# Strassen's products for the first six chunks of the down projections of a two-layer decoder trunk

## The chip, the cores and the metric

The kernel runs on one core of one Trainium2 chip. The metric is device microseconds (us) of one execution, as the median of several runs. The changed kernel is compared with the kernel before on the same chip. Engines are called PE (TensorE, matrix products), ACT (ScalarE), DVE (VectorE), POOL (GpSimd) and SP (SyncE, which issues the loads).

## The reference

Two layers (L = 2) act on x of 256 tokens by 1024 channels, in fp32. Each layer is an FFN, a token mixing and a second FFN, with a layer norm behind each. The change touches the FFNs alone, four in all:

```python
def swiglu(x, w_gate, w_up, w_down):
    return (jax.nn.silu(x @ w_gate) * (x @ w_up)) @ w_down
...
    for l in range(DEPTH):
        x = layer_norm(ALPHA * x + 0.5 * swiglu(x, ffn1_gate[l], ffn1_up[l], ffn1_down[l]),
                       ln1_g[l], ln1_b[l])
        ...
        x = layer_norm(ALPHA * x + 0.5 * swiglu(x, ffn2_gate[l], ffn2_up[l], ffn2_down[l]),
                       ln3_g[l], ln3_b[l])
```

The FFN's hidden width is 2816, so w_down is 2816 by 1024.

## The kernel before

**Precision.** Every fp32 operand a of a large product is split into a rounded part hi and a rest lo, both of type float32r. A product is then three matmuls (`mm3`, L185 to L187): hi with hi, hi with lo, lo with hi. ACT makes hi by a cast (L162 for weights, L200 for activations), DVE makes lo by a subtraction (L163, L200).

**Weights.** All weights come in one stream of tiles of 128 x 1024 in the order of a plan. `ensure` loads the next tile into one of five `raw` buffers (SP issues the load), splits it into one of twelve `hi` and one of twelve `lo` buffers, and runs seven tiles ahead of the tile that PE asks for.

**An FFN.** The hidden width is cut into a chunk 0 of 512 and chunks 1 to 9 of 256. For chunk 0, gate and up are computed with tokens on the partitions (`tok`: 128 x 512 matmuls for each half t of the tokens), then h = silu(gate) * up is transposed on PE (`trans`, tile `tr`). For chunks 1 to 9, `chan` computes gate (`pg`) and up (`pu`) with the channels on the partitions, 48 matmuls of 128 x 256 each; ACT makes `sg` = silu(pg) (L350), DVE makes h = pu * sg (L355), and h is split into `hTh` and `hTl`. `down` adds a chunk's share of h @ w_down to four PSUM tiles `y` (two halves of the tokens by two halves of the 1024 output columns): for each block of 128 hidden rows 2 x 2 products of 128 x 512, three matmuls each.

**Order.** A scheduler fixes each engine's order of instructions when the program is built. Within the step of chunk c, PE computes gate c, then a share of the down projection of earlier chunks, then up c. The down share of a step is 24 matmuls in most steps; chunks 6 to 9 are taken at the end of the FFN. In the trace each engine's instructions start in that order, so one that waits holds up those behind it.

**PSUM.** There are eight banks: two for `gu` (gate and up take turns), two for `tr`, four for `y`.

Of the kernel before, what the change touches and what calls it, by code (L numbers as in the profile page):

```python
# [7 lines left out]
F32 = mybir.dt.float32  # L8
F32R = mybir.dt.float32r
# [8 lines left out]
S = 256  # L18
# [5 lines left out]


CHUNKS = [(0, 512)] + [(512 + 256 * i, 256) for i in range(9)]


def _w_in_groups():
# [92 lines left out]
def _build(tc, A, out):  # L122
# [3 lines left out]
    with ExitStack() as es:  # L126
# [6 lines left out]
        sm = pool("sm", 3)  # L133
        lnp = pool("lnp", 1)
        ps = pool("ps", 2, space=PSUM)


        plan = _plan()
# [6 lines left out]
        loaded = []  # L145
        splits = []
        stream = []

        def ensure(i):
# [177 lines left out]
        def ffn(l, f, lni, last=False, mid=None):  # L327
            n = len(CHUNKS)
            y = {}
            started = set()  # L330
            products = []

            def tok(name, t, tag="gu", bufs=2, ahead=None):

                w = kslices((l, f, name, 0), 512, ahead)
                p = ps.tile([128, 512], F32, name="p" + name, tag=tag, bufs=bufs)
                products[:] = [mm3(p, xT(t, k), w[k], k == 0, k == KC - 1) for k in range(KC)]
                return p

            def chan(name, c):  # L340

                w = kslices((l, f, name, c), 256)
                p = ps.tile([128, 2, 256], F32, name="p" + name, tag="gu")
                proj_chan(p, w, 0)
                return p


            def gated(p):
                sg = wk.tile([128, 512], F32, name="sg", tag="w")
                ACT.activation(sg, p.rearrange("p a b -> p (a b)") if len(p.shape) == 3 else p, AF.Silu)  # L350
                return sg

            def product(p, sg):
                h = wk.tile([128, 512], F32, name="h", tag="w")
                DVE.tensor_tensor(h, p.rearrange("p a b -> p (a b)") if len(p.shape) == 3 else p, sg, ALU.mult)  # L355
                return h

            hT = {}

            def hpair():  # L360
                return (wk.tile([128, 512], F32R, name="hTh", tag="a"),
                        wk.tile([128, 512], F32R, name="hTl", tag="a"))

            def trans(h, t):
                tr = ps.tile([128, 512], F32, name="tr", tag="tr")
                for i in range(4):
                    c = slice(i * 128, i * 128 + 128)
                    PE.transpose(tr[:, c], h[:, c], ident)
                hT[0, t] = hpair()
                split_to(*hT[0, t], tr)  # L370

            def stationary(c, t, i):
                if c == 0:
                    s = slice(i * 128, i * 128 + 128)
                    a = hT[0, t]
                else:
                    s = slice(i * 256 + t * 128, i * 256 + t * 128 + 128)
                    a = hT[c]
                return a[0][:, s], a[1][:, s]

            def down(cs, t, end=False):

                todo = [(c, i, nn) for c in cs for i in range(CHUNKS[c][1] // 128) for nn in range(2)]
                if end:
                    todo.sort(key=lambda v: v[2])
                if t not in y:
                    y[t] = [ps.tile([128, 512], F32, name="y", tag="y", bufs=4) for _ in range(2)]
                done = []
                for j, (c, i, nn) in enumerate(todo):
                    hi, lo = blocks((l, f, "d", c))[i]  # L390
                    s = slice(nn * 512, nn * 512 + 512)
                    stop = end and (j == len(todo) - 1 or todo[j + 1][2] != nn)
                    done.append(mm3(y[t][nn], stationary(c, t, i), (hi[:, s], lo[:, s]), (t, nn) not in started, stop))
                    started.add((t, nn))
                return done

            h = {}
            if l == 0 and f == 1:
                sg = [gated(tok("g", 0, "y", 4, ahead=0))]
# [4 lines left out]
                sg.append(gated(tok("g", 1, "y", 4)))  # L404
                h = {t: product(tok("u", t), sg[t]) for t in range(2)}
                trans(h[0], 0)
            else:
                for t in range(2):
                    sg = gated(tok("g", t))
                    if t == 1:  # L410
                        trans(h[0], 0)
                    h[t] = product(tok("u", t), sg)


            late = 4
            for c in range(1, n):
                p = chan("g", c)
                sg = gated(p)
                if c == 1:
                    trans(h[1], 1)  # L420
                    down([0], 0)
                elif c == 2:
                    down([0], 1)
                    down([1], 0)
                else:
                    if c - 2 < n - late:
                        down([c - 2], 1)
                    if c - 1 < n - late:
                        down([c - 1], 0)
                hc = product(chan("u", c), sg)  # L430
                hT[c] = hpair()
                split_to(*hT[c], hc)
                if c == 2:
                    with tc.issue_after(stream[-1].ins):
                        gb = load_ln(l, lni)
                if c == 4 and mid:
                    with tc.issue_after(stream[-1].ins):
                        mid()
            down(range(n - late, n - 1), 0)
            down([n - 1], 0, end=True)  # L440
            done = down(range(n - late, n), 1, end=True)
            layer_norm(0, y[0], 2 * ALPHA, 4 * EPS, gb, last, [done[9], done[14]])
            layer_norm(1, y[1], 2 * ALPHA, 4 * EPS, gb, last)


        def mixing(l, sp):
            gbn = load_ln(l, 1)

            def token_proj(key, n, t):
                w = kslices((l, key), n)  # L450
                p = ps.tile([128, 512], F32, name="pt", tag="gu")
                for k in range(KC):
                    mm3(p[:, :n], xT(t, k), w[k], k == 0, k == KC - 1)
                return p

            def chan_proj(key, n, b0, ahead=None):

                w = kslices((l, key), n, ahead)
                p = ps.tile([128, 2, 256], F32, name="pc", tag="gu")
                proj_chan(p, w, b0)  # L460
                return p

# [101 lines left out]
            mixl = [lop.tile([128, 8, 128], F32R, name="mixl", tag="lo") for _ in range(2)]  # L564

            def spatial():
                p = ps.tile([128, 2, 2, 128], F32, name="psv", tag="gu")
# [38 lines left out]

            yo = {}

            def w_out(t, kbs, tag, bufs, by_half):
                w = blocks((l, "wo"))  # L610
                if t not in yo:
                    yo[t] = [ps.tile([128, 512], F32, name="yo", tag=tag, bufs=bufs) for _ in range(2)]
# [117 lines left out]
            with ExitStack() as order:  # L730
# [3 lines left out]
                for i, (t, slots) in enumerate(steps):  # L734
# [14 lines left out]
                w_out(0, range(4), "gu", 2, False)  # L749
                w_out(0, range(4, 8), "gu", 2, True)  # L750
                heads_out(1)
                layer_norm(0, yo[0], ALPHA, EPS, gbn)
                w_out(1, range(8), "y", 4, True)
                layer_norm(1, yo[1], ALPHA, EPS, gbn)

        for l in range(L):
# [41 lines left out]
```

## Time and profile before

| | |
|---|---|
| median of 3 runs | 994.37 us (994.21 to 994.58) |
| the profiled execution, its own time | 993.1 us |
| its span, first to last instruction | 991.4 us |
| PE busy | 978.0 us, 99% of the span |
| DVE busy | 603.2 us, 61% |
| ACT busy | 468.4 us, 47% |
| granted TensorE clock, mean | 0.997 of full speed |

The profiled execution is 1.27 us faster than the median of the runs, and its time is 1.7 us more than its span. A busy share is the time in which an engine has some instruction in work; matmuls overlap one another, so PE's speed is read from the spacing of matmuls, not from their durations.

### The profile page before, as it was taken

What the parts mean: (1) busy time and instruction counts of PE and PEld (TensorE: products, weight loads), DVE (VectorE), ACT (ScalarE), POOL (GpSimd) and SP (SyncE); (2) the same over time, 40 slices, a digit from 0 to 9 for tenths busy, and PEclk for the clock granted to TensorE, in tenths of its full rate; (3) what the DMA queues carried; (4) which work ended last, traced back from release to release, by engine and by line L of the source; (5) the groups of instructions that cost most, each with busy time, mean ns of one, the idle gap of its engine ahead of it and who ended that gap; (6) DMA issues with size and microseconds to landing.
All of it is one profiled execution on the core that took longest, in us unless ns stands there. A gap on an engine that the chain in (4) does not pass through costs nothing.

```text
span 991.4 us, 16634 instructions
## 1 busy us (share of the span) xinstructions
PE 978.0 (99%) x6824; PEld 887.4 (90%) x6828; DVE 603.2 (61%) x830; ACT 468.4 (47%) x658; POOL 19.7 (2%) x42
## 2 busy tenths in 40 slices
PE   7999999999999999999999999999999999999996
PEld 6999999899878899999889999998988789999995
DVE  6655455686769555455584545548678785545534
ACT  6644444256655444344354444434565663534420
POOL 1000000010000000000000000000000000000000
PEclk9999999999999999999999999999999999999998
DMA  8967565385226666556375766554642265755601
GB/s 284 331 241 237 171 198 187 105 309 160 87 86 194 231 213 194 189 189 205 94 231 195 255 205 202 196 157 168 237 149 85 86 229 198 253 190 184 205 16 42
DMA packets 53067, 183.17 MB, mean 185 GB/s; under 512 B 6656, under 2 KB 7168, under 8 KB 52992
## 3 DMA queue, kind: packets, MB, share of 16 engines
q1 hardware_dynamic: 52992, 182.12, 55.2%
q8 instruction: 53, 0.87, 0.4%
q14 instruction: 22, 0.18, 0.1%
HBM read 181.05 MB, written 1.05 MB: 184 GB/s over the span
## 4 chain that ended last, share of the span: by engine, by line
PE 99%; DMA 0%; DVE 0%; issue 0%; SPq 0%; DVEq 0%; ACT 0%
PE y L185 8%; PE y L187 8%; PE y L186 8%; PE pu L195 7%; PE pg L195 7%; PE pg L197 7%; PE pu L197 7%; PE pg L196 7%; PE pu L196 7%; PE pc L195 3%; PE pc L197 3%; PE pc L196 3%; PE pg L187 2%; PE yo L187 2%; PE yo L185 2%; PE pg L185 2%
## 5 line engine op out<-in xcount | busy, mean ns | idle before, releaser
L163 DVE TENSOR_TENSOR lo<-raw,hi 128x1024 fp32r<-128x1024 f32 (+2 forms) x326 | 389.9, 1203 | 283.1 <-ACT hi L162 267.3
L162 ACT CAST hi<-raw 128x1024 fp32r<-128x1024 f32 (+2 forms) x326 | 335.1, 1037 | 385.6 <-PE pu L196 153.6
L195 PE MATMUL pu<-xTh,hi 128*128 128x256 f32 x576 | 161.3, 280 | 0.0
L195 PE MATMUL pg<-xTh,hi 128*128 128x256 f32 x576 | 161.3, 280 | 0.0
L197 PE MATMUL pu<-xTh,lo 128*128 128x256 f32 x576 | 160.8, 279 | 0.0
L197 PE MATMUL pg<-xTh,lo 128*128 128x256 f32 x576 | 160.8, 279 | 0.0
L196 PE MATMUL pu<-xTl,hi 128*128 128x256 f32 x576 | 160.8, 279 | 0.0
L196 PE MATMUL pg<-xTl,hi 128*128 128x256 f32 x576 | 160.7, 279 | 0.0
L185 PE MATMUL y<-hi,hTh 128*128 128x512 f32 x352 | 138.6, 394 | 0.0
L187 PE MATMUL y<-hi,hTl 128*128 128x512 f32 x352 | 137.4, 390 | 0.0
L186 PE MATMUL y<-lo,hTh 128*128 128x512 f32 x352 | 136.9, 389 | 0.0
L195 PEld LDWEIGHTS pu<-xTh,hi 128*128 128x128 f32 x576 | 108.1, 188 | 1.1
L196 PEld LDWEIGHTS pu<-xTl,hi 128*128 128x128 f32 x576 | 107.8, 187 | 1.1
L197 PEld LDWEIGHTS pu<-xTh,lo 128*128 128x128 f32 x576 | 108.3, 188 | 0.0
L197 PEld LDWEIGHTS pg<-xTh,lo 128*128 128x128 f32 x576 | 108.3, 188 | 0.0
L195 PEld LDWEIGHTS pg<-xTh,hi 128*128 128x128 f32 x576 | 108.1, 188 | 0.1
L196 PEld LDWEIGHTS pg<-xTl,hi 128*128 128x128 f32 x576 | 107.8, 187 | 0.1
L187 PEld LDWEIGHTS y<-hi,hTl 128*128 128x128 f32 x352 | 66.0, 188 | 14.7
L186 PEld LDWEIGHTS y<-lo,hTh 128*128 128x128 f32 x352 | 66.1, 188 | 12.6
L185 PEld LDWEIGHTS y<-hi,hTh 128*128 128x128 f32 x352 | 66.1, 188 | 12.3
L195 PE MATMUL pc<-xTh,hi 128*128 128x256 f32 x256 | 73.0, 285 | 0.0
L197 PE MATMUL pc<-xTh,lo 128*128 128x256 f32 x256 | 72.5, 283 | 0.0
(153 smaller groups left out, 1246.4 us busy)
## 6 DMA issues: line engine op xcount, KB each, us to landing
raw<-in_ws SPq DMA_DIRECT2D x312, 512.0 KB, 4.6
w<-in_ws SPq DMA_DIRECT2D x8, 512.0 KB, 6.1
lng<-in_ln SPq DMA_DIRECT2D x6, 512.0 KB, 6.7
lnb<-in_ln SPq DMA_DIRECT2D x6, 512.0 KB, 7.5
raw<-in_ws SPq DMA_DIRECT2D x8, 256.0 KB, 4.0
raw<-in_ws SPq DMA_DIRECT2D x4, 420.0 KB, 3.5
x<-in_x SPq DMA_DIRECT2D x4, 256.0 KB, 4.5
out<-x SPq DMA_DIRECT2D x4, 256.0 KB, 2.1
```

The costliest lines, as they stand in the source:

```text
L162: splits.append((ACT.copy(hi, raw), DVE.tensor_tensor(lo, raw, hi.bitcast(F32), ALU.subtract)))
L163: DVE.tensor_tensor(lo, raw, hi.bitcast(F32), ALU.subtract)))
L185: PE.matmul(o, lhsT=a[0], rhs=b[0], start=start, stop=False)
L186: PE.matmul(o, lhsT=a[0], rhs=b[1], start=False, stop=False)
L187: return PE.matmul(o, lhsT=a[1], rhs=b[0], start=False, stop=stop)
L195: PE.matmul(p[:, b, :], lhsT=hi, rhs=xTh[:, k, :], start=k == 0, stop=False)
L196: PE.matmul(p[:, b, :], lhsT=hi, rhs=xTl[:, k, :], start=False, stop=False)
L197: PE.matmul(p[:, b, :], lhsT=lo, rhs=xTh[:, k, :], start=False, stop=k == KC - 1)
```

## The change

The hidden rows of chunks 0 to 5 (`PAIRED = 6`) are taken as seven pairs of 128-row blocks. With the two halves of the tokens and the two halves of the output columns, each pair is a 2 x 2 by 2 x 2 block product. Before, it was eight block products. Now it is Strassen's seven (in Winograd's form), M1 to M7, of three matmuls of 128 x 512 each, and each Mi is summed over all seven pairs in a PSUM bank of its own.

- **Weights** (`pair_operands`): the two raw tiles of a pair are not only split; DVE also takes four differences of half tiles, in place in the raw buffers, and splits what results. One half tile and three whole tiles are split, in place of two whole tiles. The raw buffers are held until the last of these splits.
- **Left side** (`left_sums`): for each pair DVE makes four sums of 128 x 128 blocks of h, and ACT and DVE split them (tile `S`). Chunk 0's h is copied from PSUM first (`hf`).
- **Order**: in step c, `paired` puts M1, M2, M4 of chunk c - 1 between gate and up, and M5, M6, M7, M3 behind up. Chunk 0 has two pairs, so its step has twice as many.
- **PSUM**: M1, M2, M4, M5 take the four `y` banks, M6 and M7 the `tr` banks, M3 one of the `gu` banks. Gate and up of chunks 1 to 6 share the one bank that is left (`free`).
- **`combine`**: behind chunk 5's products, DVE adds the seven sums into x in eleven instructions of 128 x 512, and ACT copies one. The layer norm then takes x with factor 1. Chunks 6 to 9 are computed as before, into `y`.
- `sg` and h get a higher priority in the scheduler, and the `gu` banks elsewhere are named in turn (`gu_bank`).

```diff
--- before.py
+++ after.py
...
                 src = A["ws"][o:o + 128 * n].rearrange("(p c) -> p c", p=128)
+                if len(key) == 4 and key[2] == "d" and key[3] < PAIRED:
+                    raw = rawp.tile([128, n], F32, name="raw", tag="raw")
+                    stream.append(SP.dma_start(raw, src))
+                    if k % 2 == 0:
+                        loaded.append(raw)
+                    else:
+                        loaded[-1] = pair_operands(loaded[-1], raw)
+                        loaded.append(loaded[-1])
+                    continue
...
+
+        def pair_operands(ra, rb):
+
+            a, b = slice(0, 512), slice(512, 1024)
+            sub = lambda o, i, j: DVE.tensor_tensor(o, i, j, ALU.subtract)
+            pairs_loaded.append(1)
+            odd = len(pairs_loaded) % 2
+            w1 = (hip, lop)[odd].tile([128, 1024], F32R, name="b11", tag=("hi", "lo")[odd])
+            split_to(w1[:, a], w1[:, b], ra[:, a])
+
+            def both(r):
+                hi = hip.tile([128, 1024], F32R, name="hi", tag="hi")
+                lo = lop.tile([128, 1024], F32R, name="lo", tag="lo")
+                split_to(hi, lo, r)
+                return hi, lo
+
+            bh, bl = both(rb)
+            sub(ra[:, a], ra[:, b], ra[:, a])
+            sub(ra[:, b], rb[:, b], ra[:, b])
+            th, tl = both(ra)
+            sub(rb[:, b], rb[:, b], ra[:, a])
+            sub(rb[:, a], rb[:, b], rb[:, a])
+            sh, sl = both(rb)
+            return {1: (w1[:, a], w1[:, b]), 2: (bh[:, a], bl[:, a]), 3: (bh[:, b], bl[:, b]),
+                    4: (sh[:, a], sl[:, a]), 5: (th[:, a], tl[:, a]), 6: (sh[:, b], sl[:, b]),
+                    7: (th[:, b], tl[:, b])}
...
             def chan(name, c):
 
                 w = kslices((l, f, name, c), 256)
-                p = ps.tile([128, 2, 256], F32, name="p" + name, tag="gu")
+                if c <= PAIRED:
+                    p = ps.tile([128, 2, 256], F32, name="p" + name, tag=free, bufs=1)
+                else:
+                    p = gu_bank([128, 2, 256], "p" + name)
                 proj_chan(p, w, 0)
                 return p
...
                     c = slice(i * 128, i * 128 + 128)
                     PE.transpose(tr[:, c], h[:, c], ident)
                 hT[0, t] = hpair()
-                split_to(*hT[0, t], tr)
+                hf[t] = wk.tile([128, 4, 128], F32, name="hf", tag="w")
+                ACT.copy(hf[t].rearrange("p a b -> p (a b)"), tr)
+                split_to(*hT[0, t], hf[t].rearrange("p a b -> p (a b)"))
...
+            left = {}
+            M = {}
+
+            def left_sums(c, i, a11, a12, a21, a22):
+
+                S = wk.tile([128, 4, 128], F32, name="S", tag="w")
+                DVE.tensor_tensor(S[:, 0, :], a21, a22, ALU.add)
+                DVE.tensor_tensor(S[:, 1, :], S[:, 0, :], a11, ALU.subtract)
+                DVE.tensor_tensor(S[:, 2, :], a11, a21, ALU.subtract)
+                DVE.tensor_tensor(S[:, 3, :], a12, S[:, 1, :], ALU.subtract)
+                hi, lo = hpair()
+                split_to(hi, lo, S.rearrange("p a b -> p (a b)"))
+                part = lambda j: (hi[:, j * 128:j * 128 + 128], lo[:, j * 128:j * 128 + 128])
+                left[c, i] = {5: part(0), 6: part(1), 7: part(2), 3: part(3)}
+
+            def left_side(c, i, m):
+                if m in (3, 5, 6, 7):
+                    return left[c, i][m]
+                t, b = {1: (0, 0), 2: (0, 1), 4: (1, 1)}[m]
+                if c:
+                    return stationary(c, t, b)
+                s = slice((2 * i + b) * 128, (2 * i + b) * 128 + 128)
+                return hT[0, t][0][:, s], hT[0, t][1][:, s]
+
+            def paired(c, ms):
+
+                for m in ms:
+                    if m not in M:
+                        tag, bufs = {3: (held, 1), 6: ("tr", 2), 7: ("tr", 2)}.get(m, ("y", 4))
+                        M[m] = ps.tile([128, 512], F32, name=f"M{m}", tag=tag, bufs=bufs)
+                    for i in range(CHUNKS[c][1] // 256):
+                        w = blocks((l, f, "d", c))[2 * i]
+                        mm3(M[m], left_side(c, i, m), w[m], c == 0 and i == 0,
+                            c == PAIRED - 1 and i == CHUNKS[c][1] // 256 - 1)
+
+            def combine():
+
+                add = lambda o, i, j: DVE.tensor_tensor(o, i, j, ALU.add)
+                q = [[x[t][:, n * 512:n * 512 + 512] for n in range(2)] for t in range(2)]
+                scaled = lambda o, m, op: DVE.scalar_tensor_tensor(o, o, 2 * ALPHA, m, ALU.mult, op)
+                scaled(q[0][1], M[3], ALU.add)
+                u = wk.tile([128, 512], F32, name="u", tag="w")
+                ACT.copy(u, M[1])
+                scaled(q[0][0], M[1], ALU.add)
+                add(q[0][0], q[0][0], M[2])
+                add(u, u, M[6])
+                add(q[0][1], q[0][1], M[5])
+                add(q[0][1], q[0][1], u)
+                add(u, u, M[7])
+                scaled(q[1][0], M[4], ALU.subtract)
+                add(q[1][0], q[1][0], u)
+                scaled(q[1][1], M[5], ALU.add)
+                add(q[1][1], q[1][1], u)
 
...
-
-            late = 4
+            turns.append(1)
+            free, held = f"gu{len(turns) % 2}", f"gu{1 - len(turns) % 2}"
             for c in range(1, n):
                 p = chan("g", c)
-                sg = gated(p)
+                with tc.high_priority(offset=60):
+                    sg = gated(p)
                 if c == 1:
                     trans(h[1], 1)
-                    down([0], 0)
-                elif c == 2:
-                    down([0], 1)
-                    down([1], 0)
-                else:
-                    if c - 2 < n - late:
-                        down([c - 2], 1)
-                    if c - 1 < n - late:
-                        down([c - 1], 0)
-                hc = product(chan("u", c), sg)
+                    for i in range(2):
+                        a = lambda t, b: hf[t][:, 2 * i + b, :]
+                        left_sums(0, i, a(0, 0), a(0, 1), a(1, 0), a(1, 1))
+                if c <= PAIRED:
+                    paired(c - 1, (1, 2, 4))
+                pu = chan("u", c)
+                with tc.high_priority(offset=60):
+                    hc = product(pu, sg)
+                if c <= PAIRED:
+                    paired(c - 1, (5, 6, 7, 3))
                 hT[c] = hpair()
                 split_to(*hT[c], hc)
+                if c < PAIRED:
+                    a = lambda t, b: hc[:, b * 256 + t * 128:b * 256 + t * 128 + 128]
+                    left_sums(c, 0, a(0, 0), a(0, 1), a(1, 0), a(1, 1))
+                if c == PAIRED:
+                    combine()
                 if c == 2:
                     with tc.issue_after(stream[-1].ins):
                         gb = load_ln(l, lni)
                 if c == 4 and mid:
                     with tc.issue_after(stream[-1].ins):
                         mid()
-            down(range(n - late, n - 1), 0)
+
+            down(range(PAIRED, n - 1), 0)
             down([n - 1], 0, end=True)
-            done = down(range(n - late, n), 1, end=True)
-            layer_norm(0, y[0], 2 * ALPHA, 4 * EPS, gb, last, [done[9], done[14]])
-            layer_norm(1, y[1], 2 * ALPHA, 4 * EPS, gb, last)
+            done = down(range(PAIRED, n), 1, end=True)
+            layer_norm(0, y[0], 1.0, 4 * EPS, gb, last, [done[9], done[14]])
+            layer_norm(1, y[1], 1.0, 4 * EPS, gb, last)
```

First, DVE in the middle of the first FFN, steps of chunks 4 and 5: before, the time between two h's is filled with splits of weights (six tiles a step). A row names the line, the operation, out<-in, the shape, and the engines and queues that it waits for.

```order
L163 TENSOR_TENSOR lo<-raw,hi 128x1024 [waits DMAHW6_49,PE_49,Activation_49]
L355 TENSOR_TENSOR h<-pu,sg 128x512 [waits PE_49]
L163 TENSOR_TENSOR lo<-raw,hi 128x1024 [waits DMAHW7_49,Activation_49]
L200 TENSOR_TENSOR hTl<-h,hTh 128x512 [waits Activation_49]
L163 TENSOR_TENSOR lo<-raw,hi 128x1024 [waits DMAHW0_49,PE_49,Activation_49]
```

The same place now, from one h on (L187 is the split of an ordinary weight tile, L250 a split by `split_to`, with b_1220 the half tile of M1, L193 a difference of weights, L441 to L444 the sums of the left side):

```order
L411 TENSOR_TENSOR h<-pu,sg 128x512 [waits PE_49]
L250 TENSOR_TENSOR b_1220<-raw,b_1220 128x512 [waits DMAHW2_49,Activation_49]
L441 TENSOR_TENSOR S<-h 128x128 [waits DVE_49]
L250 TENSOR_TENSOR hTl<-h,hTh 128x512 [waits Activation_49]
L442 TENSOR_TENSOR S<-S,h 128x128 [waits DVE_49]
L443 TENSOR_TENSOR S<-h 128x128
L444 TENSOR_TENSOR S<-h,S 128x128 [waits DVE_49]
L193 TENSOR_TENSOR raw<-raw 128x512
L250 TENSOR_TENSOR lo<-raw,hi 128x1024 [waits DMAHW2_49,Activation_49]
L250 TENSOR_TENSOR hTl<-S,hTh 128x512 [waits Activation_49]
L193 TENSOR_TENSOR raw<-raw 128x512 [waits DVE_49] x3
L250 TENSOR_TENSOR lo<-raw,hi 128x1024 [waits Activation_49] x2
```

Four ordinary splits (L187) follow, of the next chunk's gate and up, and then the next h. ACT's order in the same step is: `sg`, four casts of gate and up weights, the cast for M1's half tile, the cast of h, the cast of the pair's second tile, the cast of S, the two casts of differences, and the next `sg`.

Second, PE at the start of the first FFN, behind the up products of chunk 0. Before, the gate of chunk 1 follows the transposes of the first half of h:

```order
L187 MATMUL pu<-hi,xTl 128x512
L368 MATMUL tr<-ident,h 128x128 [waits DVE_49]
L368 MATMUL tr<-ident,h 128x128 x3
L195 MATMUL pg<-xTh,hi 128x256 [waits Activation_49]
L196 MATMUL pg<-xTl,hi 128x256
```

Now both halves of h are transposed and chunk 0's M1 (M_529) and M2 (M_536) stand ahead of that gate, twelve matmuls in all; M4 to M3 come later, as in the other steps:

```order
L237 MATMUL pu<-hi,xTl 128x512
L424 MATMUL tr<-ident,h 128x128 [waits DVE_49]
L424 MATMUL tr<-ident,h 128x128 x3
L424 MATMUL tr<-ident,h 128x128 [waits DVE_49]
L424 MATMUL tr<-ident,h 128x128 x3
L235 MATMUL M_529<-b_250,hTh 128x512 [waits Activation_49]
L236 MATMUL M_529<-b_250,hTh 128x512
L235 MATMUL M_536<-hi,hTh 128x512
L236 MATMUL M_536<-lo,hTh 128x512
L237 MATMUL M_529<-b_250,hTl 128x512 [waits DVE_49]
```

Third, DVE at that same place, from the second pair of chunk 0 to the first gate tile of chunk 1 (L187, the last row). Before, the seven rows between two h's here were ordinary splits and one hTl:

```order
L250 TENSOR_TENSOR b_300<-raw,b_300 128x512 [waits DMAHW2_49,Activation_49]
L250 TENSOR_TENSOR lo<-raw,hi 128x1024 [waits DMAHW3_49,Activation_49]
L193 TENSOR_TENSOR raw<-raw 128x512 [waits DVE_49]
L411 TENSOR_TENSOR h<-pu,sg 128x512 [waits PE_49]
L193 TENSOR_TENSOR raw<-raw 128x512 [waits DVE_49]
L250 TENSOR_TENSOR hTl<-hf,hTh 128x512 [waits Activation_49]
L193 TENSOR_TENSOR raw<-raw 128x512 [waits DVE_49]
L250 TENSOR_TENSOR lo<-raw,hi 128x1024 [waits Activation_49]
L193 TENSOR_TENSOR raw<-raw 128x512 [waits DVE_49]
L250 TENSOR_TENSOR lo<-raw,hi 128x1024 [waits Activation_49]
L187 TENSOR_TENSOR lo<-raw,hi 128x1024 [waits DMAHW4_49,Activation_49]
```

The first gate tile of chunk 1 now stands behind both pairs of chunk 0 on DVE, and behind their casts on ACT.

Behind M3 of chunk 5, PE's next instructions are 16 matmuls of the up product of chunk 7, in the bank `free`, and then the gate of chunk 7 in the bank that M3 held. Of `combine`, M3's addition is the third on DVE, behind those of M4 and M1.

The order of PE's instructions in the token mixing is the same in both kernels.

## Rows read from the trace of the kernel before

**Rows 1.** The page: busy us by engine; the chain that ended last, by engine.

```profile
PE 978.0 (99%) x6824; PEld 887.4 (90%) x6828; DVE 603.2 (61%) x830; ACT 468.4 (47%) x658; POOL 19.7 (2%) x42
...
PE 99%; DMA 0%; DVE 0%; issue 0%; SPq 0%; DVEq 0%; ACT 0%
```

**Rows 2.** All waits of PE in the program: us, times, longest.

```profile
PE tr L217 <- POOL blk L267: 3.6, 1, 3.6
PE tr L217 <- DMA x<-in_x: 1.4, 1, 1.4
```

**Rows 3.** Chain, step of chunk 5 in FFN 1: start, us, what.

```profile
108.56 0.24 PE y L185
...
114.04 0.12 PE pu L195
...
119.69 0.12 PE pg L195
...
125.35 0.24 PE y L185
```

**Rows 4.** The same step by engines: busy us (instructions), clock, DMA share, GB/s.

```profile
108.60:125.40 16.80, 16.80 (x121) 15.81 (x120) 8.47 (x9) 7.36 (x9) 0.00 (x0) 1.00 0.59 190
```

**Rows 5.** Groups by form: busy us, mean ns, idle before.

```profile
L163 DVE TENSOR_TENSOR lo<-raw,hi 128x1024 fp32r<-128x1024 f32 x312 | 379.1, 1222 | 271.6 <-ACT hi L162 255.7 <-DMA w<-in_w 11.3
L162 ACT CAST hi<-raw 128x1024 fp32r<-128x1024 f32 x312 | 325.5, 1052 | 373.3 <-PE pu L196 153.6 <-PE pg L196 78.5 <-PE y L187 54.7
...
L355 DVE TENSOR_TENSOR h<-pu,sg 128x512 f32<-128x512 f32 x44 | 30.1, 685 | 11.1 <-PE pu L197 8.2 <-PE pu L187 2.8
...
L350 ACT ACTIVATE sg<-pg 128x512 f32<-128x512 f32 x44 | 26.0, 591 | 4.7 <-PE pg L197 3.6 <-PE pg L187 1.0
...
L200 ACT CAST hTh<-h 128x512 fp32r<-128x512 f32 x36 | 22.4, 622 | 21.2 <-DVE h L355 21.2
```

**Rows 6.** DVE in order of time, in that step and in the mixing.

```profile
119.33 1.23 DVE L163 TENSOR_TENSOR lo<-raw,hi 128x1024 fp32r<-128x1024 f32 x1 [5.66 <-ACT hi L162]
120.47 0.68 DVE L355 TENSOR_TENSOR h<-pu,sg 128x512 f32<-128x512 f32 x1
121.07 1.22 DVE L163 TENSOR_TENSOR lo<-raw,hi 128x1024 fp32r<-128x1024 f32 x1
...
277.76 0.28 DVE L650 TENSOR_TENSOR pcm<-pcm,c 128x128 f32<-128x128 f32 x1
277.96 0.20 DVE L649 RECIPROCAL csum<-csum 128x8 f32<-128x8 f32 x1
```

**Rows 7.** Loads of raw tiles in steps of chunks 4 and 5.

```profile
DMA to landing us min/median/max: 3.5/4.5/5.0
```

**Rows 8.** Start of FFN 1: DVE and ACT in order of time, PE in the chain.

```profile
18.14 7.07 DVE L163 TENSOR_TENSOR lo<-raw,hi 128x1024 fp32r<-128x1024 f32 x6 [0.25 <-ACT hi L162]
...
27.54 0.68 DVE L355 TENSOR_TENSOR h<-pu,sg 128x512 f32<-128x512 f32 x1
...
33.41 0.68 DVE L355 TENSOR_TENSOR h<-pu,sg 128x512 f32<-128x512 f32 x1
...
22.89 1.06 ACT L162 CAST hi<-raw 128x1024 fp32r<-128x1024 f32 x1 [0.37 <-DMA raw<-in_ws]
...
32.16 0.44 PE tr L368 x4
```

**Rows 9.** The chain at the start; the last stretch by engines (clock after the five engines).

```profile
7.18 0.43 PE pg L185
...
10.36 0.23 PE pg L187
...
985.00:991.00 6.00, 0.00 (x0) 0.00 (x0) 3.03 (x7) 0.00 (x0) 0.92 (x1) 0.60 0.23 87
```

**Rows 10.** Start of FFN 3: last weight split of DVE before the first gate, and PE.

```profile
506.14 1.22 DVE L163 TENSOR_TENSOR lo<-raw,hi 128x1024 fp32r<-128x1024 f32 x1
...
519.93 0.28 PE L195 MATMUL pg<-xTh,hi 128*128 128x256 f32 x1
```

More of the change, by code (lines that the diff above doesn't have):

```diff
@@ L26 @@
 CHUNKS = [(0, 512)] + [(512 + 256 * i, 256) for i in range(9)]
+PAIRED = 6
 def _w_in_groups():
@@ L135, in _build, with gu_bank @@
         ps = pool("ps", 2, space=PSUM)
+        turns = []
+        def gu_bank(shape, name):
+            turns.append(1)
+            return ps.tile(shape, F32, name=name, tag=f"gu{len(turns) % 2}", bufs=1)
         plan = _plan()
@@ L147, in _build @@
         stream = []
+        pairs_loaded = []
         def ensure(i):
@@ L331, in ffn, with tok @@
             products = []
-            def tok(name, t, tag="gu", bufs=2, ahead=None):
+            def tok(name, t, in_y=False, ahead=None):
                 w = kslices((l, f, name, 0), 512, ahead)
-                p = ps.tile([128, 512], F32, name="p" + name, tag=tag, bufs=bufs)
+                if in_y:
+                    p = ps.tile([128, 512], F32, name="p" + name, tag="y", bufs=4)
+                else:
+                    p = gu_bank([128, 512], "p" + name)
                 products[:] = [mm3(p, xT(t, k), w[k], k == 0, k == KC - 1) for k in range(KC)]
@@ L342, in chan @@
                 w = kslices((l, f, name, c), 256)
-                p = ps.tile([128, 2, 256], F32, name="p" + name, tag="gu")
+                if c <= PAIRED:
+                    p = ps.tile([128, 2, 256], F32, name="p" + name, tag=free, bufs=1)
+                else:
+                    p = gu_bank([128, 2, 256], "p" + name)
                 proj_chan(p, w, 0)
@@ L379, in stationary @@
-                return a[0][:, s], a[1][:, s]
+                s = slice(i * 256 + t * 128, i * 256 + t * 128 + 128)
+                return hT[c][0][:, s], hT[c][1][:, s]
+            hf = {}
+            left = {}
[10 more added lines that the diff above has]
+                left[c, i] = {5: part(0), 6: part(1), 7: part(2), 3: part(3)}
@@ L398, in ffn @@
             if l == 0 and f == 1:
-                sg = [gated(tok("g", 0, "y", 4, ahead=0))]
+                sg = [gated(tok("g", 0, True, ahead=0))]
                 with ExitStack() as order:
@@ L403, in ffn @@
                     ensure(index[l, f, "g", 0][-1] + 3)
-                sg.append(gated(tok("g", 1, "y", 4)))
+                sg.append(gated(tok("g", 1, True)))
                 h = {t: product(tok("u", t), sg[t]) for t in range(2)}
@@ L450, in token_proj @@
                 w = kslices((l, key), n)
-                p = ps.tile([128, 512], F32, name="pt", tag="gu")
+                p = gu_bank([128, 512], "pt")
                 for k in range(KC):
@@ L458, in chan_proj @@
                 w = kslices((l, key), n, ahead)
-                p = ps.tile([128, 2, 256], F32, name="pc", tag="gu")
+                p = gu_bank([128, 2, 256], "pc")
                 proj_chan(p, w, b0)
@@ L566, in spatial @@
             def spatial():
-                p = ps.tile([128, 2, 2, 128], F32, name="psv", tag="gu")
+                p = gu_bank([128, 2, 2, 128], "psv")
                 for t in range(2):
@@ L607, in mixing, with w_out @@
             yo = {}
-            def w_out(t, kbs, tag, bufs, by_half):
+            def w_out(t, kbs, in_y, by_half):
                 w = blocks((l, "wo"))
                 if t not in yo:
-                    yo[t] = [ps.tile([128, 512], F32, name="yo", tag=tag, bufs=bufs) for _ in range(2)]
+                    yo[t] = [ps.tile([128, 512], F32, name="yo", tag="y", bufs=4) if in_y else
+                             gu_bank([128, 512], "yo") for _ in range(2)]
                 todo = [(kb, n) for kb in kbs for n in range(2)]
@@ L748, in mixing @@
                         fn()
-                w_out(0, range(4), "gu", 2, False)
-                w_out(0, range(4, 8), "gu", 2, True)
+                w_out(0, range(4), False, False)
+                w_out(0, range(4, 8), False, True)
                 heads_out(1)
                 layer_norm(0, yo[0], ALPHA, EPS, gbn)
-                w_out(1, range(8), "y", 4, True)
+                w_out(1, range(8), True, True)
                 layer_norm(1, yo[1], ALPHA, EPS, gbn)
```

7 lines of the change are left out of this document (1 added, 6 removed).

## The prediction, written before the changed kernel ran

> **What bounds the kernel now.** I read the page first: PE is busy for 99% of the span, DVE for 61%, ACT for 47%, and the chain that ended last is PE for 99% [rows 1]. Then PE's waits: in the whole program it waits for another engine for 5 us, all at the start [rows 2]. So PE has hardly a gap, and the time is the number of its matmuls times their spacing. The spacing comes from the chain through one step: 24 matmuls of 128 x 512 from 108.56 to 114.04, 0.228 us each; 48 of 128 x 256 from 114.04 to 119.69 and 48 more to 125.35, 0.1177 us each [rows 3]. In such a step of 16.8 us DVE is busy for 8.5 and ACT for 7.4 [rows 4]: there is room, but it is finite.
>
> **What the change removes.** Each pair takes 7 x 3 matmuls in place of 8 x 3, of the same form as y. Seven pairs in four FFNs: 84 matmuls less, times 0.228 = 19.15 us. All lie on the bounding chain, so this is the whole gain if PE is kept fed: 993.1 - 19.15 = 973.95 for the profiled execution, with the same 1.7 us around the span as before. The medians run 1.27 us above the profiled execution (994.37 against 993.1), so 975.2 in that measure.
>
> **What it adds.** No matmul; on DVE, per pair, one more split of a whole tile (1.22), a half tile's split, four differences, the split of S, at 0.685 each like h, and four sums of 128 x 128 (0.28): 1.22 + 6 x 0.685 + 4 x 0.28 = 6.45 us [rows 5, 6]. `combine` is 11 x 0.685 = 7.5 us per FFN. Together 28 x 6.45 + 4 x 7.5 = 211 us, so DVE goes from 603 to some 814 us, 83% of the span. ACT gains 28 x (1.05 + 2 x 0.62), 8 copies of hf and 4 of u: some 71 us, to 540. As a sum over the program this fits under PE. The question is each stage.
>
> **A step of a paired chunk (20 of them, chunks 2 to 6).** PE now needs 96 x 0.1177 + 21 x 0.228 = 16.09 us. DVE needs per step 7 splits of whole tiles, 8 operations of 512 and 4 of 128. At their durations this is 8.55 + 5.48 + 1.14 = 15.2 us. But operations in a row start closer than they last: 1.14 us for a split, 0.60 for h, 0.20 for a 128 [rows 6]; so 7 x 1.14 + 8 x 0.60 + 4 x 0.20 = 13.6 us if nothing waits. It fits, with 0.9 to 2.5 us to spare; but much of it is a chain, which I walked through by hand. Time 0 is the end of the up product. PE: M5 to M3 until 2.74, gate until 8.39, M1 to M4 until 10.44, up until 16.09. In the trace h starts 0.8 us behind that end, since a split stands before it (120.47 against 119.69) [rows 3, 6]. From there DVE: h to 1.5, M1's half tile and the first sum 2.3, hTl 2.9, three sums 3.6, a difference and the pair's second tile 5.3, S's split 5.9, three differences that each need the last 7.8; with ACT's two casts in between the splits of the differences end at 9.0 and 10.1. ACT's last cast ends at 8.9, its silu at 9.4; PE wants that bank at 10.4 (one bank for gate and up): 1.0 us spare. The next h ends at 1.5 of the next step; PE wants the bank at 2.74: 1.2 us spare. The raw tile of the pair is free at 9.0; the load for the next step's last up tile lands 4.5 us later [rows 7], 13.5; its cast and split end at 15.9, and h comes at 16.9 anyway. The round that goes through that load (h at 0.8 to the split at 15.9, 15.1 us) closes within 16.09. So I cost these steps at nothing, with about 1 us of cover; if the cover is gone, the price is the excess of the round, twenty times.
>
> **The first FFN's start** costs. Here nothing was loaded ahead, and DVE has to split chunk 0's two pairs before chunk 1's gate tile; its splits run without a gap from 18.14 [rows 8]. From there in the new order: four up tiles 22.7; first pair: half tile 23.3, two differences 24.7, second tile and first difference tile 27.0, a difference, h of the first half, a difference 28.9; then ACT's cast, 1.05, and the split: 31.2. Second pair: half tile 31.8, second tile 33.0, difference, h (before: 33.41, about as now), difference 34.8, hTl, difference, split, difference 37.8, cast, split 40.1; gate tile of chunk 1 at 41.2. PE finished the up product at 32.16 [rows 8]; it does the first transposes, waits 1.6 us for the second h (34.2), does the transposes and the twelve matmuls until 37.6, and waits 3.6 us. Then ACT: the silu of that gate stands behind two casts of chunk 1's pair, whose second raw tile can only be loaded when the gate tile's buffer is free (41.2 + 4.5); I get 2.2 us more, and 0.3 for S. Sum: 7.7 us. Bounds: if DVE ran at its spacings alone, with no hand-over to ACT (11 whole tiles and 13 operations of 512, 20.3 us), the gate tile is there at 38.5, and PE loses 3 us; with 0.1 us more at each of some 30 hand-overs, 11.
>
> **The other three starts.** Here the splits of chunk 0 begin during the layer norm before. In FFN 3 the last of these four splits ended at about 507.3 before, and PE began chunk 1's gate at 519.93 [rows 10]. Now from 506.8, behind the norm's last split: two differences, two splits of the first pair, h, the second pair, gate tile: 12.4 us, 519.2; the third matmul, which needs it, comes 2 x 0.1177 behind that start, at 520.16. Just in time. In FFN 2 and 4 the same walk ends some 0.3 us late. I take 1 us for the three together; the bounds are 0 and 7.7 each (as in the first FFN).
>
> **Behind the last pair** PE wants M3's bank, which waits for one addition on DVE (0.69). Sixteen matmuls of up 7 stand before it (16 x 0.1177 = 1.9 us) and h of chunk 6 has the bank they use; so nothing. The other ten additions lie beside gate and up 7, where DVE's splits were done a step ahead.
>
> [...]
>
> **Sum.** 993.1 - 19.15 + 7.7 + 1.0 + 1.4 = 984.05 for a profiled execution; plus 1.27: **985.3 us**, 0.9% faster. What I call no change is within 0.2% (992.4 to 996.4), about what a measurement of this kernel can tell.
>
> **Rivals.**
> - A, the forecast: steps hold, starts cost 4 to 14 us. 979 to 989. Chance 0.58.
> - B, the starts cost under 4 us, because what I took as hand-overs overlaps: 975.2 to 979. For it speaks that DVE's splits follow each other at 1.14 us without loss [rows 6]. Chance 0.10.
> - C, the round of a paired step is longer than PE's 16.09: DVE becomes the bound there. Its place is the raw tile that waits for the pair's differences. If each of eight hand-overs between DVE and ACT takes 0.15 us and loads take 5.0 us [rows 7], the round is 15.1 + 1.2 + 0.5 = 16.8, and 20 x 0.7 = 14 us are lost: 999. The point of decision is 16.54: there 20 x 0.45 us eat what the starts leave of the gain (9.1). Against it: all rounds are below 16.09 by rows. Chance 0.20, 988 to 1010; half of it slower, 0.06 no change, 0.04 faster.
> - D, every FFN starts as badly as the first: 4 x (7.7 + 1.4) = 36 us against 19: 975.2 + 36.4 = 1011.6. For it: DVE is as busy in those stretches, since the layer norm's work stands between. Chance 0.12.
>
> Faster: 0.58 + 0.10 + 0.04 = 0.72; same 0.06; slower 0.10 + 0.12 = 0.22. The range 977 to 1001 leaves out D, the end of C and half of B; A's own is 979 to 989.
>
> **What would show it.** 84 matmuls fewer; M1 of successive chunks 16.1 us apart in FFN 1 (C: 16.8 or more, with PE waiting for h or sg). PE's waits: the gate of chunk 1 in FFN 1 for a weight split, 3 to 4 us near 40 us, and the up product behind it for sg; the same lines in FFN 2 to 4 under 1 us (D: 7). DVE busy near 814 us. I would be wrong if the waits in the paired steps repeat, or if a load that I did not follow (the layer norm's gains, in step 2, and the mixing's small ones, in step 4, go through SP's same queue) delays a raw tile by over 1 us.

## The result

The changed kernel takes 1003.07 us (median of four runs, 1000.13 to 1004.12) against 994.3 beside it: 1.0083 times as long (95% interval 1.0059 to 1.0107), 0.8% slower, where 0.9% faster was forecast. Its profiled execution took 1002.03 us with a span of 1000.3, 8.9 more than before.

The page of the changed kernel: busy us by engine, then the chain that ended last, by engine and the head of it by line.

```profile
PE 967.6 (97%) x6744; PEld 873.5 (87%) x6744; DVE 784.2 (78%) x1182; ACT 527.7 (53%) x754; POOL 19.0 (2%) x42
...
PE 68%; DVE 13%; DMA 11%; ACT 5%; issue 3%; SPq 0%; ACTq 0%; DVEq 0%
DMA raw<-in_ws 10%; PE pu L245 5%; PE pu L246 5%; PE pu L247 5%; DVE raw L193 4%; PE pg L245 4%; PE pg L247 4%; PE pg L246 4%; DVE lo L250 3%; PE y L237 3%; PE y L235 3%; PE y L236 3%; PE pc L245 3%; PE pc L247 3%; PE pc L246 3%
```

Against [rows 1] the chain is no longer PE alone: about a third of it runs through DVE, ACT and the loads of raw tiles, which are its largest single line. What PE waits for (us, times, longest); before it was 5 us at the very start and nothing else [rows 2]:

```profile
PE pu L245 <- ACT sg L406: 11.4, 12, 2.5
...
PE pg L245 <- ACT hi L186: 2.2, 1, 2.2
PE tr L424 <- DVE h L411: 1.8, 1, 1.8
PE pg L247 <- DVE lo L187: 0.9, 1, 0.9
PE pg L245 <- DVE h L411: 0.9, 1, 0.9
PE M L237 <- DVE hTl L250: 0.6, 1, 0.6
```

Twelve waits are for the silu, which must read the gate's bank before the up product takes it (in a paired step both use one bank). Here is a ledger from PE's timeline, each FFN from its first gate product (in FFN 1 from that of the second row tile) to the start of its last stretch of down products. From each, 4.79 us should have gone (21 matmuls at 0.228):

| | before | changed | difference | lost of the gain |
|---|---|---|---|---|
| FFN 1 | 14.82 to 173.00, 158.18 | 16.14 to 185.10, 168.96 | +10.78 | 15.6 |
| FFN 2 | 309.19 to 473.47, 164.28 | 321.19 to 484.51, 163.32 | -0.96 | 3.8 |
| FFN 3 | 496.21 to 660.47, 164.26 | 507.24 to 671.13, 163.89 | -0.37 | 4.4 |
| FFN 4 | 797.32 to 961.61, 164.29 | 808.11 to 970.55, 162.44 | -1.85 | 2.9 |

The rest of the 8.9 us lies ahead of PE's second gate product, which began 1.3 us later: 0.8 of it is the first x tile, which landed later (2.2 us of waiting against 1.4), and the other 0.5 was not taken apart. The change need not be its reason: over the traces kept, of either kernel and of their variants, that product begins anywhere from 14.54 to 17.38 us. Within FFN 1, from that gate product to the up product of chunk 1 takes 34.52 us (16.14 to 50.66) against 29.19 before (14.82 to 44.01), in which 24 down products (5.57) stood where 12 (2.75) stand now: 8.1 us are lost at the start, 7.4 behind it. In the other FFNs the starts lose 1.1 us together, and the paired steps the rest, about 10.

The steps show it: PE's timeline in FFN 3, the first M1 product of four successive chunks.

```profile
557.94 0.40 PE L235 MATMUL M<-b,hTh 128*128 128x512 f32 x1
...
574.09 0.40 PE L235 MATMUL M<-b,hTh 128*128 128x512 f32 x1
...
591.51 0.40 PE L235 MATMUL M<-b,hTh 128*128 128x512 f32 x1
...
608.67 0.40 PE L235 MATMUL M<-b,hTh 128*128 128x512 f32 x1
```

The intervals are 16.15, 17.42 and 17.16, where 16.09 was forecast. What a long one (the last) is made of is read from the chain between two silus there (start, us, what):

```profile
576.70 0.59 ACT sg L406
577.29 0.95 ACT hi L186
...
578.26 1.24 DVE lo L187
...
579.51 5.23 DMA raw<-in_ws
...
584.84 1.06 ACT hi L250
...
585.92 1.23 DVE lo L250
587.15 0.60 DVE hTl L250
587.75 0.20 DVE S L441
...
588.35 0.60 DVE raw L193
...
589.80 0.69 DVE raw L193
590.49 0.60 DVE hTl L250
591.09 1.14 DVE lo L250
592.23 0.61 DVE raw L193
...
592.92 1.06 ACT hi L250
```

and the silu that follows, in ACT's own order of time:

```profile
593.87 0.59 ACT L406 ACTIVATE sg<-pg 128x512 f32<-128x512 f32 x1
```

The silu is followed in ACT's order by the cast of the next chunk's first gate tile; its split frees a raw buffer; that buffer is the one that the **second tile of the pair** waits for (six tiles a step, five buffers); the load takes 5.23 us; the tile is cast and split; then come the sums of S with the first three differences among and behind them, the splits of S and of the first difference tile, the fourth difference, the cast of the last difference tile at 592.92, and right behind it in ACT's order the next silu. The round is 593.87 - 576.70 = 17.17 us, and PE can't go round in 16.09. DVE itself stands idle in it for 1.55 us until 585.92.

Where the norm's gains are loaded, the load in that round is longer still. SP's queue at that place of FFN 1:

```profile
71.37 0.33 SPq L170 DMA_DIRECT2D raw<-in_ws  x1
71.74 0.43 SPq L342 DMA_DIRECT2D lng<-in_ln  x1
72.22 0.42 SPq L343 DMA_DIRECT2D lnb<-in_ln  x1
72.80 0.33 SPq L170 DMA_DIRECT2D raw<-in_ws  x1
```

and the chain there:

```profile
72.80 8.33 DMA raw<-in_ws
```

The gains stand between the two tiles of a pair, and the second lands after 8.33 us in place of 5.23. The round at this place is 17.26 us all the same (silus at 69.98 and 87.24): the tile lands so late that the sums of S and one difference are done by then, and less stands behind the landing. The longest rounds are 19.60 us at the gains of FFN 2 (silus at 372.23 and 391.83, a load of 9.39) and 18.89 us at the mixing's seven small loads in FFN 1 (104.96 and 123.85).

### The profile page after: what moved, and what is told of

It reads as the page before. It is cut to its first block, busy times and chain, and to the rows that moved or that the text cites. A ratio compares the mean times of both kernels' runs of the same rounds, so it can differ in the third digit from the quotient of the medians.

```text
span 1000.3 us, 16957 instructions
## 1 busy us (share of the span) xinstructions
PE 967.6 (97%) x6744; PEld 873.5 (87%) x6744; DVE 784.2 (78%) x1182; ACT 527.7 (53%) x754; POOL 19.0 (2%) x42
## 4 chain that ended last, share of the span: by engine, by line
PE 68%; DVE 13%; DMA 11%; ACT 5%; issue 3%; SPq 0%; ACTq 0%; DVEq 0%
DMA raw<-in_ws 10%; PE pu L245 5%; PE pu L246 5%; PE pu L247 5%; DVE raw L193 4%; PE pg L245 4%; PE pg L247 4%; PE pg L246 4%; DVE lo L250 3%; PE y L237 3%; PE y L235 3%; PE y L236 3%; PE pc L245 3%; PE pc L247 3%; PE pc L246 3%
## 5 line engine op out<-in xcount | busy, mean ns | idle before, releaser
L187 DVE TENSOR_TENSOR lo<-raw,hi 128x1024 fp32r<-128x1024 f32 (+2 forms) x270 | 316.9, 1198 | 75.8 <-ACT hi L186 71.2
L186 ACT CAST hi<-raw 128x1024 fp32r<-128x1024 f32 (+2 forms) x270 | 271.4, 1032 | 185.4 <-PE y L237 46.0
L245 PE MATMUL pu<-xTh,hi 128*128 128x256 f32 x576 | 163.1, 283 | 11.5 <-ACT sg L406 11.4
L250 ACT CAST hi<-raw 128x1024 fp32r<-128x1024 f32 x84 | 87.7, 1051 | 90.5 <-DVE raw L193 52.9
L250 DVE TENSOR_TENSOR lo<-raw,hi 128x1024 fp32r<-128x1024 f32 x84 | 101.9, 1219 | 27.9 <-ACT hi L250 27.5
L193 DVE TENSOR_TENSOR raw<-raw 128x512 f32<-128x512 f32 x112 | 76.9, 687 | 3.3 <-DMA raw<-in_ws 1.6
L246 PE MATMUL pc<-xTl,hi 128*128 128x256 f32 x256 | 71.6, 280 | 0.0
L237 PE MATMUL M<-hi,hTl 128*128 128x512 f32 x168 | 66.0, 393 | 0.6 <-DVE hTl L250 0.6
L235 PE MATMUL M<-hi,hTh 128*128 128x512 f32 x168 | 66.2, 394 | 0.0
```

The source lines that it names most:

```text
L186: splits.append((ACT.copy(hi, raw), DVE.tensor_tensor(lo, raw, hi.bitcast(F32), ALU.subtract)))
L193: sub = lambda o, i, j: DVE.tensor_tensor(o, i, j, ALU.subtract)
L235: PE.matmul(o, lhsT=a[0], rhs=b[0], start=start, stop=False)
L237: return PE.matmul(o, lhsT=a[1], rhs=b[0], start=False, stop=stop)
L245: PE.matmul(p[:, b, :], lhsT=hi, rhs=xTh[:, k, :], start=k == 0, stop=False)
L246: PE.matmul(p[:, b, :], lhsT=hi, rhs=xTl[:, k, :], start=False, stop=False)
```

## The experiments

Three theories. **R**: the round through the pair's second raw buffer is longer than PE's step. **S**: only the silu's place in ACT's order, behind the casts of the differences, is at fault. **Q**: only the small loads between the two tiles of a pair are. The traces tell them apart by the intervals of M1: 16 of them lie between the successive paired steps of the four FFNs, and their excess over 16.09 us sums to 16.7 us in the changed kernel (here and below from one profiled execution each). Times are medians; "before" is the kernel before on the same chip, 993.98 in the first four runs and 994.58 in the others.

**One buffer more.**

```
-        rawp = pool("raw", 5)
+        rawp = pool("raw", 6)
```

> Edit: six raw buffers in place of five, nothing else. Theory R (the round through the raw buffers is longer than PE's 16.09 us: silu to silu 17.17 us in FFN 3, through a cast, a split, a load of 5.23, the pair's split, sums, differences and casts): the pair's second tile no longer waits for the split of the gate tile behind the silu (2.8 us after the silu begins) but for that of the previous pair's second tile (about 1.2 us after it), so the round shortens by some 1.6 us to 15.6, below 16.09, and PE's waits for the silu go in the steps that hold no other loads: 990 to 996 us. Theory S (only the place of the silu in ACT's order, behind the two casts of the difference tiles, whenever the tile lands): no change against the changed kernel, 1000 to 1004. Theory Q (the norm's gains and the mixing's small loads in SP's queue between the two tiles of a pair): the loads stand where they did, so 999 to 1003.

Measured: 984.34 us, 0.9903 of before (0.9888 to 0.9917). R said 990 to 996, so even R was too cautious: the start of FFN 1 gained too. The casts stand before the silu from step 3 on as they did, and the small loads where they did, so S and Q, which forecast 999 to 1004, fall as sole causes. The steps nearly close: the excess of the 16 intervals falls from 16.7 to 4.6 us. PE's waits:

```profile
PE pu L245 <- ACT sg L406: 3.1, 5, 0.8
...
PE pg L247 <- DVE lo L187: 0.5, 1, 0.5
PE tr L424 <- DVE h L411: 0.3, 1, 0.3
```

**Two buffers more**, paid for with work buffers.

```
-        rawp = pool("raw", 5)
+        rawp = pool("raw", 7)
-        wk = pool("wk", 9)
+        wk = pool("wk", 8)
```

> Edit: seven raw buffers; eight work buffers of each kind in place of nine, to make room. Theory R: the pair's second tile waits for the split of the previous pair's first, another 2 us earlier; the round is near 13.5 us, and even loads of 8 to 9 us behind the norm's gains nearly fit: 984 to 991 us. Theory S: 1000 to 1004. Theory Q: the extra loads of 4 to 6 us are covered in part: 994 to 999.

Measured: 980.83 us, 0.9863 of before (0.9847 to 0.9879). PE waits for one silu in the whole program:

```profile
PE pu L245 <- ACT sg L406: 0.7, 1, 0.7
```

SP's issue of a pair's second tile in FFN 3, the silu of that step (chunk 4), and two successive M1:

```profile
575.71 0.33 SPq L170 DMA_DIRECT2D raw<-in_ws  x1
...
577.33 0.59 ACT L406 ACTIVATE sg<-pg 128x512 f32<-128x512 f32 x1
...
576.15 0.40 PE L235 MATMUL M<-b,hTh 128*128 128x512 f32 x1
...
592.29 0.40 PE L235 MATMUL M<-b,hTh 128*128 128x512 f32 x1
```

and that issue in the same step of the changed kernel, whose silu stands at 593.87 (above):

```profile
599.01 0.36 SPq L170 DMA_DIRECT2D raw<-in_ws  x1
```

The engines over four paired steps there (PE, PEld, DVE, ACT, POOL busy, then the clock):

```profile
552.00:617.00 65.00, 65.00 (x471) 61.35 (x471) 55.58 (x74) 37.41 (x44) 0.81 (x1) 1.00 0.70 237
```

The second tile of the pair is now issued 1.6 us before the silu (575.71 against 577.33), with the mixing's small loads ahead of it; in the changed kernel it was issued 5.1 us behind it in this step (599.01 against 593.87), and 2.8 us in the step before (579.51 against 576.70). PE is busy for 65.00 of 65.00 us with DVE at 55.58, so DVE's work as such was not the bound of these steps: all sums, differences and splits are still there. The intervals of M1 are 16.14 to 16.15 in all four FFNs (excess 0.9 us in all). FFN 2 lasts 159.76 us (310.66 to 470.42), 4.52 shorter than before.

**The small loads moved** from steps 2 and 4 to 7 and 8, five buffers.

```
-                if c == 2:
+                if c == 7:
                     with tc.issue_after(stream[-1].ins):
                         gb = load_ln(l, lni)
-                if c == 4 and mid:
+                if c == 8 and mid:
```

> Edit: the gains of the norm are loaded in step 7 in place of 2, the mixing's small tensors in step 8 in place of 4, so that nothing stands between the two tiles of a pair in SP's queue. Theory Q: the waits that follow loads of 8 to 9 us go (0.6 and 1.3 us in FFN 1 behind the gains, 2.5 and a stretch of lower clock of 1.7 behind the mixing's, 0.9 and 0.9 in FFN 2, 1.0 and 1.2 in FFN 3, 1.1 in FFN 4, and what the pipelined ends hide of them): 989 to 993 us. Theory R: only the added delay goes, rounds with a load of 5.2 us still last 17.2: 995 to 1000. Theory S: no change, 1000 to 1004.

Measured: 991.8 us (987.96 to 994.12 over ten runs), 0.9974 of before (0.9963 to 0.9985). That is Q's number, not R's: the loads made 11 of the lost us. The excess of the 16 intervals falls from 16.7 to 6.8 us, so the small loads made the larger part of what the steps lost, and the round with ordinary loads the smaller. But the steps don't close: intervals of 17.47, 17.30, 17.03 and 17.38 us are left, the longest of each FFN, with no such load near, and PE still waits for the silu:

```profile
PE pu L245 <- ACT sg L406: 5.2, 7, 1.1
```

**The silu ahead of the difference tiles**, five buffers: the four differences run together, and `rest` (the casts and splits of the two difference tiles) is issued behind the silu.

```
-            th, tl = both(ra)
             sub(rb[:, b], rb[:, b], ra[:, a])
             sub(rb[:, a], rb[:, b], rb[:, a])
-            sh, sl = both(rb)
...
+                with tc.issue_after(sg_ins[0].ins):
+                    for rest in behind:
+                        rest()
```

> Edit: the four differences of a pair run together, and the casts and splits of its two difference tiles are issued behind the silu of the step, not ahead of it. Theory S: the silu starts when the gate product ends, PE's waits for it go: 988 to 994 us. Theory R: the silu leaves the round but both tiles of a pair are held 2 to 3 us longer, so the casts of later tiles come late in its place: 996 to 1003. Theory Q: 997 to 1003.

Measured: 995.29 us (992.03 to 998.19 over ten runs), 1.001 of before (0.9997 to 1.0023): 1.3 us beyond S's range and 0.7 below R's, so the time decides nothing. The trace (of the fastest run) does: the M1 intervals of FFN 2 to 4 are 16.14 to 16.15, so with the silu out of the round it closes even with five buffers, and the small loads where they were. R had expected the casts of later tiles to come late in the silu's place; in these steps they don't. The silu's place is a link of the round, but no wait by itself (ring6 left it). What stays is the start of FFN 1 and a few waits, the longest of 2.1 us for the silu of FFN 1's chunk 6; the other nine runs have no trace. PE's waits, whose lines stand nine further down in this kernel:

```profile
PE pu L254 <- ACT sg L417: 5.0, 4, 2.1
...
PE M L244 <- ACT hTh L259: 2.3, 3, 0.9
PE pg L254 <- ACT hi L187: 2.2, 1, 2.2
PE tr L435 <- DVE h L422: 1.8, 1, 1.8
```

**The seven buffers in the kernel before**, as a control.

```
-        rawp = pool("raw", 5)
+        rawp = pool("raw", 7)
-        wk = pool("wk", 9)
+        wk = pool("wk", 8)
```

> Edit, of the kernel before the change: seven raw buffers and eight work buffers of each kind, as in ring7. Theory R: PE waits for no load in the kernel before, so more raw buffers are worth nothing there: 993 to 995.5 us (at most 0.1 to 0.2% either way, from the first loads). Rival: what ring7 gave (23 us under the changed kernel) is in part a gain that any kernel with these pools has: then 985 to 992.

Measured: 994.56 us, 1.0004 (0.9995 to 1.0014). The buffers are worth nothing by themselves; the 22 us that they gave the changed kernel they give only together with the change.

**The four differences left out**, five buffers.

```
             bh, bl = both(rb)
-            sub(ra[:, a], ra[:, b], ra[:, a])
-            sub(ra[:, b], rb[:, b], ra[:, b])
             th, tl = both(ra)
-            sub(rb[:, b], rb[:, b], ra[:, a])
-            sub(rb[:, a], rb[:, b], rb[:, a])
             sh, sl = both(rb)
```

> Edit: five raw buffers as in the changed kernel, and the four subtractions that make the difference tiles are left out (the tiles are split as loaded, so the output is not the reference's; matmuls, loads, casts, splits and sums are all there). Theory R: the round through the pair's second tile falls by those differences that stand on it, three of 0.6 to 0.7 us and one hand-over, from 17.17 to about 14.9, below 16.09; the steps close except behind the gains and the mixing's loads, which add 3 to 4 us once each: 985 to 992 us. Theory Q: the waits follow the extra loads alone, and these stand where they did: 995 to 1001. Rival H (the twelve hi and lo buffers, which now hold 1.6 steps of weights in place of 2, are what is short): no change but for the start, 997 to 1003.

Measured: 984.47 us, 0.9896 (0.9879 to 0.9913), a little better than R's range; PE waits for no silu at all, with as many loads, buffers, casts and small loads as in the changed kernel, and the excess of the 16 intervals is 1.1 us. H (too few hi and lo buffers) falls. But the run does not single out the differences: the scheduler made another order without them. On ACT, casts of three ordinary tiles (L186) now stand between those of the pair's tiles and the silu, so that the first gate tile's cast no longer comes behind the silu:

```profile
588.17 1.04 ACT L246 CAST hi<-raw 128x1024 fp32r<-128x1024 f32 x1
589.12 1.05 ACT L186 CAST hi<-raw 128x1024 fp32r<-128x1024 f32 x1
...
593.87 0.58 ACT L402 ACTIVATE sg<-pg 128x512 f32<-128x512 f32 x1
```

So two links of the round are gone at once, and PE's order at the start of FFN 1 is another too. Behind the first x tiles PE waits for the first FFN's h and, in a mixing, once for DVE:

```profile
PE tr L420 <- DVE h L407: 3.7, 1, 3.7
...
PE pc L241 <- DVE kd L601: 0.2, 1, 0.2
```

**Seven buffers and the moved loads.** Both edits above together.

> Edit: the two edits ring7 and late together. Theory R: with seven buffers the steps already close at 16.1 us with the extra loads where they are, so moving these gives nothing: 979.5 to 982 us. Theory Q: each load of 8 to 9 us still costs something that the wait table does not show: 975 to 979.

Measured: 981.13 us, 0.9862 (0.9846 to 0.9878), as ring7 (980.83): with seven buffers, loads of that kind in the queue cost nothing.

**Seven chunks paired**, on top of that.

```
-PAIRED = 6
+PAIRED = 7
-            layer_norm(0, y[0], 1.0, 4 * EPS, gb, last, [done[9], done[14]])
+            layer_norm(0, y[0], 1.0, 4 * EPS, gb, last, [done[9], done[11]])
```

> Edit: ring7_late with seven chunks paired in place of six: four pairs more in the program, 12 matmuls of 128x512 less, 2.7 us; the last stretch of down products has three chunks in place of four, and what the norm's transposes stand behind is cut from the 10th and 15th of sixteen products to the 10th and 12th of twelve. If that stretch still covers the norm: 977 to 979.5 us. If the norm or the combination of the seven sums, one step later, is late for it: 980 to 988.

Measured: 978.82 us, 0.9839 (0.9824 to 0.9854): 2.3 of the 2.7 us arrive, and one new wait, for the norm's split of x, costs 0.6. It is the fastest kernel here, 1.6% faster than the one before.

```profile
PE pg L237 <- DVE xTl L250: 0.6, 1, 0.6
```

## Why the prediction was wrong, point by point

- **The gain of 19.15 us** was right: with seven buffers FFN 2, 3 and 4 are each 4.5 us shorter, of 4.79.
- **DVE's and ACT's sums** were right enough: 784 against 814 and 528 against 540, since operations in a row start closer than they last (three splits of 1.22 us take 3.50 from 578.26 on).
- **The paired step, costed at nothing, is the step that failed.** I found room on DVE (55.58 of 65.00 us busy bears that out) and followed one round, from the pair's first freed buffer to the next up tile; I took the pair's second tile as landed by the time DVE wanted it. It had not landed: its own buffer came from a split that stands behind the silu, and the round from silu to silu is 17.17 us, not 16.09. Where the sum had nothing, the 16 intervals of M1 hold 16.7 us. One buffer more brings that to 4.6, two more to 0.9, the silu ahead of the difference tiles to 2.0; the control shows that the buffers give nothing without the change. Without the differences it is 1.1, but there the silu's place changed with them.
- **The small loads in SP's queue**, which I named as a risk and gave no price, made the load of a pair's second tile up to 4.2 us longer where they stand between the two tiles (9.39 against 5.23), and the round up to 19.60 us. Moving them gave 11 us and took 10 of the 16.7.
- **FFN 1's start**: 8.1 us against 7.7 + 1.4, the sum's term for the clock. The waits for h (1.8) and for the gate tile (3.1) are near the 1.6 and 3.6 forecast; that for the silu (0.7) is well under 2.2, so part of the agreement is luck. The reason was half right: with seven buffers and the same DVE operations the same stretch (16.59 to 46.28, 29.69 us) loses 3.3, about my lower bound of 3; the other 4.8 go with more buffers. That DVE's work makes the 3.3 is not shown.
- **The other starts**: 1.1 against 1.0. **The last pair's bank**: PE never waits for it. Rival D is out.
- **The clock**: the sum's term of 1.4 us is shown by no run. What the changed kernel showed in its place is a granted clock (it stands behind the five engines) of 0.83 over 10 us in FFN 1's start, and of 0.83 again over 10 us around the wait of 2.5 us near 124, for which the sum had nothing. In each, three whole microseconds read 0.50 (43 to 46 and 125 to 128), and matmuls of 128 x 256 stood 0.214 us apart there, against 0.118 where it read 1.00 (47 to 50). My estimate from the two means: 10 x (1 - 0.83) = 1.7 us lost each time.

```profile
40.00:50.00 10.00, 7.72 (x48) 7.32 (x48) 9.31 (x10) 6.71 (x8) 0.00 (x0) 0.83 0.81 277
120.00:130.00 10.00, 7.53 (x42) 6.83 (x41) 8.60 (x10) 6.47 (x7) 0.00 (x0) 0.83 0.48 161
```

- **Rival C** had the place (the raw tile that waits for the pair's differences), and its range of 988 to 1010 holds the time. It was wrong in calling DVE the bound: the bound is the latency of a round of five buffers. That its 14 us for the steps are near the 16.7 measured is partly luck, as it had no price for the small loads, which made 10 of them.

The waits for the silu did not come in every step: twelve make 11.4 us in the changed kernel, five 3.1 with six buffers, one 0.7 with seven.

What stays open: ring7's median is 5.6 us above 975.2. Its profiled execution is 7.2 us above 973.95: 3.9 in FFN 1 (157.25 us against 153.39), 1.8 ahead of its second gate product, 0.8 in the other FFNs together and 0.7 elsewhere; no run took these apart. Why sgfirst spreads over 6 us is not known.

## What to carry to other kernels

Where a change makes a tile stay longer in its buffer, follow the buffer, not the engine: write down which tile takes it next, what stands between its release and that tile's use, and close the round once for **each** tile of the step; with five buffers and six tiles a step, the last tile waits for the first of the same step. Then close it a second time with the longest load that the trace has behind other loads of the same queue. The sum of an engine's work says nothing about such a round; one buffer more was worth 18.7 us here, start of FFN 1 included, nearly all that the removed matmuls are worth (19.15).

## What the runs showed that I had not expected

- A load of 512 KB (median 4.6 us) took 8.33 (72.80) where 1 MB of gains had been issued just ahead of it in the same queue. Whether another engine's queue would have kept the gains out of the way, no run here shows.
- The kernels that have loads on the path spread more: 1000.1 to 1004.1 over four runs of the changed kernel, 988.0 to 994.1 over ten with the moved loads, against 993.2 to 995.3 over 36 runs of the kernel before. That the loads are the reason is not shown.
- The granted clock read 0.83 over 10 us where waits of 1.8, 2.2 and 0.9 us had come within 9 us (40 to 50), and where one of 2.5 had (120 to 130). Around a single wait of 0.9 us it read 1.00, and no run shows why; FFN 2 at 383:

```profile
380.00:390.00 10.00, 9.08 (x63) 8.20 (x62) 7.46 (x13) 3.77 (x5) 0.00 (x0) 1.00 0.75 292
```
